# A decoder block's down phases: left factors pinned in VectorE's order, GpSimd taken out of the first down phase, the last product's operands loaded during three products

## The chip, the core and the metric

The kernel runs on one core of a Trainium2 chip: TensorE (PE, matrix products), VectorE (DVE) and ScalarE (ACT) and GpSimd (POOL) for element work, and SyncE (SP), whose queue issues nearly all DMA transfers. The metric is the device time of one execution in microseconds (us), the median of several runs.

## The reference

One layer of a decoder: `x` is 2048 tokens by 1024 features in float32. A mixer sub-layer (attention and a gated convolution) comes first and is not touched here. The part that matters is the gated MLP and the closing norm:

```python
h = rms_norm(x, norm2_g[l]) * (1.0 + sc2) + sh2
u = h @ w_up[l]                       # 1024 -> 2 * 2816
gate, val = u[..., :D_FF], u[..., D_FF:]
f = jax.nn.silu(causal_dwconv3(gate, ffn_conv_w[l], ffn_conv_b[l])) * val
x = x + g2 * (f @ w_down[l])          # 2816 -> 1024
...
return rms_norm(x, final_norm_g)
```

## The kernel before

After the mixer the 2048 tokens are treated in two halves (`hf` 0 and 1), each with an up phase (`h @ w_up`) and a down phase (`f @ w_down`): up 0, down 0, up 1, down 1. Every matrix product is done with seven block products instead of eight, and every float32 operand is split into a rounded high part (written by ScalarE, line 337) and the rest (a subtraction on VectorE or GpSimd, line 338), so that one logical matmul is three of TensorE's.

**Left factors.** An up phase needs 28 tiles `S`, its left factors: for each of four values of `kp`, seven sums and differences of normed activations, each split in two. `left_steps` makes them. For the second half they are made during down 0: it loads four tiles of `x1d` (the residual in DRAM) into `u`, `ta`, `ta` and `tb`, scales them with the norm (line 772), forms sums and differences (777, 782, 785, and 788 on GpSimd), and splits them (758, 759; for two of the seven the split's second part is on GpSimd). `beside`, called once in each step of down 0, advances this generator.

**Down phase.** It has seven products (`i` 0 to 6) of 11 steps (`k`). A step takes a pair of tiles `op` (high and low parts, each with a left block and a right block) made by `down_step`: two loads of 256 KB into a tile `wr` (lines 1095, 1096), the high part on ScalarE, the low part on VectorE or, for each fourth step, on GpSimd. There are 3 tiles `wr` and 8 tiles `op` (four pairs). The pair of a step is asked for three steps ahead (`AHEAD`). A step is 12 matmuls into four PSUM banks. The last product of down 1 differs: its eleven pairs go into tiles of the tag `S` (28 of them, no longer needed by then), all are kept, and TensorE goes through them bank by bank. They are asked for after the last step's pair of product 5, since `todo` is one list in order of `i` and `k`.

**Closing norm.** `final` squares and sums the finished columns, `rstd_cols` makes 1/rms, `spread2` spreads it over the partitions with a matmul into the one PSUM bank `aux`, copies it by ScalarE (739) into a tile, and line 1118 multiplies eight tiles with it and sends them out.

**Order.** TensorE's instructions stay in the order of the program (`keep_in_program_order`). Those of the other engines are put in an order at build time by a scheduler that weighs them against its own estimates; at run time each engine and the SP queue go strictly through their lists.

Of the kernel before, what the change touches and what calls it, by code (L numbers as in the profile page):

```python
# [8 lines left out]
F32 = mybir.dt.float32  # L9
# [3 lines left out]
ALU = mybir.AluOpType  # L13
# [7 lines left out]
T = 512  # L21
# [36 lines left out]
def build(nc, tc, cst, pp, dr, xT, pos, pk_d, c_d, ada_d, w_in, w_o, w_up, w_dn, outT):  # L58
# [7 lines left out]
    def mm(*a, **k):  # L66
        i = nc.tensor.matmul(*a, **k)  # L67
        if static[0]:
            tc.keep_in_program_order(i)
# [662 lines left out]
    def spread2(r4, tag, gtag='nq'):  # L732
        g = t(gtag)
        vec.tensor_tensor(out=g.rearrange("p (m t) -> p m t", m=4), in0=ident.unsqueeze(1).to_broadcast([128, 4, 128]),
                          in1=r4.unsqueeze(2).to_broadcast([128, 4, 128]), op=ALU.mult)
        p = aux_tile()
        mm(p, ones, g, start=True, stop=True)
        r = t(tag)
        act(r, p, AF.Copy)
        return r  # L740
# [8 lines left out]
    def left_steps(hf, SL, rb=None):  # L749
        for n in ('11', 's1', '12', 's2', 's4', 's3', '22'):  # L750
            SL[n] = []

        def put(n, src, bias=None):
            o = t('S', dt=F32R)
            if bias is None or rb is None:
                split(o[:, W], o[:, L], src, pool if n in ('s4', 's3') and rb is not None else vec)
            else:
                act(o[:, W], src, AF.Identity, bias=bias)
                vec.scalar_tensor_tensor(out=o[:, L], in0=src, scalar=bias, in1=o[:, W].bitcast(F32),  # L759
                                         op0=ALU.add, op1=ALU.subtract)  # L760
            SL[n].append(o)

        for kp in range(4):
            A = {}
            b0, b1, b01 = sh2[:, kp:kp + 1], sh2[:, kp + 4:kp + 5], sh12[:, kp:kp + 1]
            for n, b, hk, tag in (('11', 0, 0, 'u'), ('21', 1, 0, 'ta'), ('22', 1, 1, 'ta'), ('12', 0, 1, 'tb')):
                k = kp + 4 * hk
                a = A[n] = t(tag)
                c0 = (2 * hf + b) * T
                dma(a, (h2d if rb is None else x1d)[k][:, c0:c0 + T])  # L770
                if rb is not None:
                    vec.scalar_tensor_tensor(out=a, in0=a, scalar=s2[:, k:k + 1], in1=rb[b], op0=ALU.mult, op1=ALU.mult)
                if n == '11':
                    put('11', a, b0)
                yield
            z = t('tb')
            vec.tensor_tensor(out=z, in0=A['21'], in1=A['22'], op=ALU.add)
            put('s1', z, b01)
            yield
            put('12', A['12'], b1)  # L780
            yield
            vec.tensor_tensor(out=z, in0=z, in1=A['11'], op=ALU.subtract)
            put('s2', z, b1)
            yield
            vec.tensor_tensor(out=A['12'], in0=A['12'], in1=z, op=ALU.subtract)
            put('s4', A['12'])
            yield
            (vec if rb is None else pool).tensor_tensor(out=A['21'], in0=A['11'], in1=A['21'], op=ALU.subtract)
            put('s3', A['21'])
            yield  # L790
            put('22', A['22'], b1)
            yield
# [15 lines left out]
    for q in range(NQ):  # L808
# [81 lines left out]
        for dp in range(4):  # L890
            if dp == 3:
                ps += [ps_tile(tg) for tg in ('pv', 'ps')]
                out_half(q, ps, 0, 3, ya8)
            out_half(q, ps, 1, dp, yc8)
            for d in (2 * dp, 2 * dp + 1):
                out_res(q, ps[d], d, ss2)
                if q == NQ - 1:
                    for _ in range(5):
                        next(ls, None)
    out_pool.close()  # L900
    right_pool, _ = open_pool("fb", "left", {'op': (1024, 8), 'x2': (512, 8), 'nq': (512, 2), 'wr': (1024, 3)})
# [196 lines left out]
        split(hi, lo, raw, eng)  # L1098
        return hi, lo

    def final(hf, b, x2, tag, rtag):
        s = t(tag)
        order = [(d + 4 * b) % 8 for d in range(8)]
        for i, d in enumerate(order):
            if i == 0:
                act(s, x2[d], AF.Square)
            else:
                q = t(tag)
                act(q, x2[d], AF.Square)
                vec.scalar_tensor_tensor(out=s, in0=q, scalar=EPS * D / 128 if i == 1 else 0.0, in1=s,  # L1110
                                         op0=ALU.add, op1=ALU.add)
            yield
        r = rstd_cols(s, D)
        yield
        r = spread2(r, rtag, tag)
        yield
        for d in order:
            vec.scalar_tensor_tensor(out=x2[d], in0=x2[d], scalar=col('gf', d), in1=r, op0=ALU.mult, op1=ALU.mult)  # L1118
            c0 = (2 * hf + b) * T
            dma(outT[d][:, c0:c0 + T], x2[d])  # L1120
            yield
# [3 lines left out]

    def down_phase(hf, hook, ops):

        todo = [(i, k) for i in range(7) for k in range(KH)][len(ops):]
        count = itertools.count()

        def nxt():
            if todo:
                ops.append(down_step(hf, *todo.pop(0), pool if next(count) % 4 == 3 else vec))

        for _ in range(AHEAD - len(ops)):
            nxt()
        out = {}, {}
        fin = [final(hf, 0, out[0], 'u', 'u'), final(hf, 1, out[1], *(('nq', 'nq') if hf == 0 else ('ta', 'tb')))]
        sets = [None, None]
        reads = []  # L1140

# [4 lines left out]
        n = 0  # L1146
        for i, (st, _, _, c) in enumerate(DOWN):
# [11 lines left out]
            for k in range(KH):  # L1159
                if at_end:  # L1160
                    break
                hi, lo = ops.pop(0)
                for p in range(4):
                    wc = slice(T + p * 128, T + (p + 1) * 128)
                    mm(ps[p], hi[:, wc], hi[:, W], start=(fresh and k == 0), stop=False, skip_group_check=True)
                    mm(ps[p], hi[:, wc], lo[:, W], start=False, stop=False, skip_group_check=True)
                    mm(ps[p], lo[:, wc], hi[:, W], start=False, stop=(k == KH - 1 and i in (1, 5, 6)),
                       skip_group_check=True)
                if reads:
                    read(*reads.pop(0))  # L1170
                nxt()
                if hf == 1 and i == 5:
                    nxt()
                if i == 2 and 5 <= k < 9 or i == 6:
                    next(fin[0], None)
                if i == 6 and k >= 6:
                    next(fin[0], None)
                if i == 5 and 5 <= k < 9:
                    next(fin[1], None)
                hook(n)  # L1180
                n += 1
            reads, done = [(ps[p], c, p) for p in range(4)], reads
        if hf == 1:
            while todo:
                nxt()
            for p in range(4):
                wc = slice(T + p * 128, T + (p + 1) * 128)
                for k, (hi, lo) in enumerate(ops):
                    mm(ps[p], hi[:, wc], hi[:, W], start=False, stop=False, skip_group_check=True)
                    mm(ps[p], hi[:, wc], lo[:, W], start=False, stop=False, skip_group_check=True)  # L1190
                    mm(ps[p], lo[:, wc], hi[:, W], start=False, stop=(k == KH - 1), skip_group_check=True)
# [30 lines left out]
    SL, R = {}, {}  # L1222
    rs = right_steps(0, R)
    ls = []
    NLEFT = 44

    def beside(n):
        if n == 2:
# [81 lines left out]
```

## Time and profile before

| what | us |
|---|---|
| median of 3 runs (2240.96 to 2241.58) | 2240.99 |
| the profiled execution's own time | 2238.82 |
| its span, first to last instruction | 2237.0 |
| TensorE busy in the span | 2058.7 |
| VectorE busy | 1592.7 |
| GpSimd busy | 532.9 |

The profile is of one execution, 2.17 us below the median; its time is 1.8 us more than its span. TensorE is busy for 92% of the span, so what can be won is mostly in the places where it waits, and in the stretches after such waits in which its clock is low.

### The profile page before, as it was taken

The numbers are of one execution on the slowest core, as the hardware profiler recorded it, in microseconds if no ns is written. First come the engines' busy times: TensorE is split into PE (matmuls) and PEld (weight loads), VectorE is DVE, ScalarE is ACT, GpSimd is POOL, SyncE is SP. The second block draws the span as 40 slices with busy tenths as digits, with TensorE's granted clock in tenths as the row PEclk, the third lists the DMA queues.
The fourth block names the chain that finished last, engine by engine and source line by source line (L and its number), as shares of the span: only waits on it lengthen the run. The fifth ranks groups of instructions, "written<-read, shape, count | busy, mean of one in ns | idle before, by whom it ended". The sixth has DMA issues, their size and how long they took to land.

```text
span 2237.0 us, 26087 instructions
## 1 busy us (share of the span) xinstructions
PE 2058.7 (92%) x8914; PEld 1646.0 (74%) x8914; DVE 1592.7 (71%) x2589; ACT 985.9 (44%) x1719; POOL 532.9 (24%) x306
## 2 busy tenths in 40 slices
PE   4877968988998997999999998999999999999996
PEld 3765757766777775877887877787788888878874
DVE  8897548747854759888888868758877777654454
ACT  3564435435533534544444434544544444434341
POOL 5264410000000001323323323423232323212220
PEclk7998989999999998999999999999999999999997
DMA  7674776677667556545345566665433232256662
GB/s 284 208 257 144 268 252 244 231 255 249 213 215 241 171 177 228 181 149 178 138 172 171 188 202 191 195 198 178 156 104 109 90 112 100 99 175 201 190 203 97
DMA packets 164918, 414.80 MB, mean 185 GB/s; under 512 B 19248, under 2 KB 23344, under 8 KB 152240
## 3 DMA queue, kind: packets, MB, share of 16 engines
q1 hardware_dynamic: 164640, 413.02, 54.5%
q8 instruction: 70, 1.15, 0.2%
q14 instruction: 64, 0.52, 0.1%
q10 hardware_dynamic: 144, 0.11, 0.0%
HBM read 304.52 MB, written 100.93 MB: 181 GB/s over the span
## 4 chain that ended last, share of the span: by engine, by line
PE 44%; DVE 4%; DMA 3%; issue 1%; ACT 1%; SPq 0%; POOL 0%; DVEq 0%; ACTq 0%; POOLq 0%
PE ps L67 21%; PE sc L67 12%; PE tr L67 7%; PE aux L67 2%; PE pv L67 1%; DVE op L338 1%; DMA wr<-tt 1%; DVE S L759 1%; DMA u<-x1d 0%; DMA wr<-w_dn 0%; ACT op L337 0%; DMA tb<-x1d 0%; DMA y<-x1d 0%; DVE x L1118 0%; DMA f<-u 0%
## 5 line engine op out<-in xcount | busy, mean ns | idle before, releaser
L338 POOL TENSOR_TENSOR op<-wr,op 128x512 fp32r<-128x512 f32 (+1 forms) x123 | 240.3, 1954 | 1221.6 <-DVE o L338 585.9
L67 PE MATMUL ps<-h,w 128*128 128x512 f32 x1632 | 425.6, 411 | 37.1 <-ACT rq L496 15.1
L67 PE MATMUL ps<-S,op 128*128 128x512 f32 x1584 | 389.9, 399 | 21.8 <-ACT op L337 11.5
L67 PEld LDWEIGHTS ps<-h,w 128*128 128x128 f32 x1632 | 311.3, 195 | 115.6 <-ACT rq L496 17.7
L67 PEld LDWEIGHTS ps<-S,op 128*128 128x128 f32 x1584 | 299.1, 189 | 98.8 <-ACT op L337 14.7
L337 ACT ACTIVATE op<-wr 128x1024 fp32r<-128x1024 f32 (+1 forms) x229 | 205.1, 896 | 254.6 <-PE sc L67 85.2
L338 DVE TENSOR_TENSOR op<-wr,op 128x1024 fp32r<-128x1024 f32 x106 | 140.4, 1327 | 135.8 <-ACT op L337 135.8
L1007 DVE SCALAR_TENSOR_TENSOR u<-G,pk,u 128x512 f32<-128x512 f32 x176 | 156.5, 891 | 34.2 <-ACT u L1004 32.6
L67 PE MATMUL sc<-S,op 128*128 128x512 f32 x528 | 131.0, 397 | 0.0
L67 PE MATMUL ps<-S,o 128*128 128x512 f32 x528 | 130.4, 395 | 0.0
L67 PE MATMUL tr<-S,op 128*128 128x512 f32 x528 | 130.3, 395 | 0.0
L67 PE MATMUL sc<-S,o 128*128 128x512 f32 x528 | 130.3, 395 | 0.0
L67 PE MATMUL ps<-op 128*128 128x512 f32 x462 | 120.0, 394 | 9.1 <-DVE op L338 4.8
L67 PE MATMUL sc<-op 128*128 128x512 f32 x462 | 118.4, 392 | 0.0
L67 PEld LDWEIGHTS sc<-S,op 128*128 128x128 f32 x528 | 99.8, 189 | 24.3
L67 PEld LDWEIGHTS sc<-S,o 128*128 128x128 f32 x528 | 99.1, 188 | 24.1
L67 PEld LDWEIGHTS tr<-S,op 128*128 128x128 f32 x528 | 99.1, 188 | 24.1
L67 PEld LDWEIGHTS ps<-S,o 128*128 128x128 f32 x528 | 99.0, 188 | 24.0
L67 PEld LDWEIGHTS ps<-op 128*128 128x128 f32 x462 | 86.6, 188 | 29.5 <-DVE op L338 5.6
L1004 ACT ACTIVATE u<-G,pk 128x512 f32<-128x512 f32 x88 | 71.4, 812 | 82.4 <-DVE G L988 80.7
L338 POOL TENSOR_TENSOR w<-wr,w 128x1024 fp32r<-128x1024 f32 x28 | 74.3, 2662 | 137.3 <-ACT w L337 116.3
L337 ACT ACTIVATE op<-ta 128x512 fp32r<-128x512 f32 x132 | 81.0, 624 | 57.6 <-PE ps L67 51.8
(315 smaller groups left out, 3533.6 us busy)
## 6 DMA issues: line engine op xcount, KB each, us to landing
w<-wd SPq DMA_DIRECT2D x72, 1024.0 KB, 5.9
wr<-w_up SPq DMA_DIRECT2D x86, 512.0 KB, 3.3
wd<-w SPq DMA_DIRECT2D x26, 1024.0 KB, 5.4
fs<-u SPq DMA_DIRECT2D x88, 256.0 KB, 2.1
wr<-fs SPq DMA_DIRECT2D x88, 256.0 KB, 2.9
wr<-tt SPq DMA_DIRECT2D x88, 256.0 KB, 3.3
f<-u SPq DMA_DIRECT2D x66, 256.0 KB, 2.0
wr<-f SPq DMA_DIRECT2D x66, 256.0 KB, 2.9
```

Of the source, the lines that this page charges most:

```text
L67: i = nc.tensor.matmul(*a, **k)
L337: act(hi, src, AF.Copy)
L338: return lo_eng.tensor_tensor(out=lo, in0=src, in1=hi.bitcast(F32), op=ALU.subtract)
L759: vec.scalar_tensor_tensor(out=o[:, L], in0=src, scalar=bias, in1=o[:, W].bitcast(F32), op0=ALU.add, op1=ALU.subtract)
L1004: act(u, G[:, 2:], AF.Identity, scale=fwh[:, 2 * NFF + j:2 * NFF + j + 1], bias=fwh[:, 3 * NFF + j:3 * NFF + j + 1])
L1007: vec.scalar_tensor_tensor(out=u, in0=G[:, i:i + T], scalar=fwh[:, i * NFF + j:i * NFF + j + 1], in1=u, op0=ALU.mult, op1=ALU.add)
```

## The change

Three things. The second half's left factors: every VectorE instruction of them is pinned in program order, nothing of them is on GpSimd any more, and the four loads of a `kp` are issued one `kp` ahead; the number of `yield`s falls (so `NLEFT` is 41 instead of 44). Down 0: all low parts on VectorE. Down 1: the eleven pairs of the last product have a list of their own and are asked for in every third step of products 3, 4 and 5. Besides, `spread2` returns the PSUM bank when it is given no tag, and `final` multiplies straight from it.

```diff
@@ spread2 @@
         mm(p, ones, g, start=True, stop=True)
+        if tag is None:
+            return p
         r = t(tag)
@@ left_steps @@
             if bias is None or rb is None:
-                split(o[:, W], o[:, L], src, pool if n in ('s4', 's3') and rb is not None else vec)
+                keep(split(o[:, W], o[:, L], src, vec))
             else:
                 act(o[:, W], src, AF.Identity, bias=bias)
-                vec.scalar_tensor_tensor(out=o[:, L], in0=src, scalar=bias, in1=o[:, W].bitcast(F32),
-                                         op0=ALU.add, op1=ALU.subtract)
+                keep(vec.scalar_tensor_tensor(out=o[:, L], in0=src, scalar=bias, in1=o[:, W].bitcast(F32),
+                                              op0=ALU.add, op1=ALU.subtract))
             SL[n].append(o)
+        def keep(x):
+            return x if rb is None else tc.keep_in_program_order(x)
+
+        def load(kp):
+            A = {}
+            for n, b, hk, tag in (('11', 0, 0, 'u'), ('21', 1, 0, 'ta'), ('22', 1, 1, 'ta'), ('12', 0, 1, 'tb')):
+                A[n] = t(tag)
+                c0 = (2 * hf + b) * T
+                dma(A[n], (h2d if rb is None else x1d)[kp + 4 * hk][:, c0:c0 + T])
+            return A
+
+        nxt = load(0)
+        yield
         for kp in range(4):
-            A = {}
+            A = nxt
...
-            vec.tensor_tensor(out=A['12'], in0=A['12'], in1=z, op=ALU.subtract)
+            if kp < 3:
+                nxt = load(kp + 1)
+            keep(vec.tensor_tensor(out=A['12'], in0=A['12'], in1=z, op=ALU.subtract))
             put('s4', A['12'])
             yield
-            (vec if rb is None else pool).tensor_tensor(out=A['21'], in0=A['11'], in1=A['21'], op=ALU.subtract)
+            keep(vec.tensor_tensor(out=A['21'], in0=A['11'], in1=A['21'], op=ALU.subtract))
             put('s3', A['21'])
@@ final @@
-        r = spread2(r, rtag, tag)
+        r = spread2(r, None, tag)
@@ down_phase @@
-        todo = [(i, k) for i in range(7) for k in range(KH)][len(ops):]
+        todo = [(i, k) for i in range(7 - hf) for k in range(KH)][len(ops):]
+        last = [(6, k) for k in range(KH)] if hf == 1 else []
+        lops = []
...
-                ops.append(down_step(hf, *todo.pop(0), pool if next(count) % 4 == 3 else vec))
+                ops.append(down_step(hf, *todo.pop(0), pool if hf == 1 and next(count) % 4 == 3 else vec))
...
                 nxt()
-                if hf == 1 and i == 5:
-                    nxt()
+                if last and i >= 3 and k % 3 == 0:
+                    lops.append(down_step(hf, *last.pop(0), pool if len(lops) % 4 == 2 else vec))
...
-            while todo:
-                nxt()
+            assert not last
...
-                for k, (hi, lo) in enumerate(ops):
+                for k, (hi, lo) in enumerate(lops):
```

Up to the first steps of down 0 all engines' lists are the same as before, and TensorE's list is the same from end to end. The lists differ at three places. The first is VectorE at the start of down 0 (`op<-wr` is a step's low part, lines 772, 777 and 759 the left factors). Before:

```order
L338 TENSOR_TENSOR op<-wr,op 128x1024 x2
L772 SCALAR_TENSOR_TENSOR tb<-tb,s_105,u 128x512
L772 SCALAR_TENSOR_TENSOR ta<-ta,s_105,u 128x512 x4
L772 SCALAR_TENSOR_TENSOR u<-u,s_105 128x512
L777 TENSOR_TENSOR tb<-ta 128x512
L772 SCALAR_TENSOR_TENSOR u<-u,s_105 128x512
L777 TENSOR_TENSOR tb<-ta 128x512
L338 TENSOR_TENSOR op<-wr,op 128x1024
L772 SCALAR_TENSOR_TENSOR tb<-tb,s_105,u 128x512
L759 SCALAR_TENSOR_TENSOR S<-u,sh_106,S 128x512
```

The same place in the changed kernel (lines 785 and 761 are the former 772 and 759, 1162 is the former 1144, which reads a finished PSUM bank):

```order
L338 TENSOR_TENSOR op<-wr,op 128x1024 x6
L785 SCALAR_TENSOR_TENSOR u<-u,s_105 128x512
L338 TENSOR_TENSOR op<-wr,op 128x1024
L785 SCALAR_TENSOR_TENSOR ta<-ta,s_105,u 128x512
L761 SCALAR_TENSOR_TENSOR S<-u,sh_106,S 128x512
L338 TENSOR_TENSOR op<-wr,op 128x1024 x2
L785 SCALAR_TENSOR_TENSOR ta<-ta,s_105,u 128x512
L1162 SCALAR_TENSOR_TENSOR y_10668<-ps,g_107,y_10668 128x512
L338 TENSOR_TENSOR op<-wr,op 128x1024
L785 SCALAR_TENSOR_TENSOR tb<-tb,s_105,u 128x512
```

Before, nine instructions of the left factors, of two values of `kp` at once, stand between two low parts; now they come one to five at a time, over the whole phase.

The second place is SP's queue in down 0, where `ta<-x1d` are left factors' loads and `wr<-` those of the steps. In the changed kernel the loads of the third `kp` stand behind the fourth step of product 2:

```order
L1111 DMA wr<-fs_115 128x512
L1112 DMA wr<-tt_126 128x512
L773 DMA ta<-x1d 128x512 x2
L1111 DMA wr<-fs_115 128x512
L1112 DMA wr<-tt_126 128x512
```

Before, the same pair of loads stood in the middle of product 1:

```order
L770 DMA ta<-x1d 128x512
L1095 DMA wr<-f_112 128x512
L1096 DMA wr<-w_dn 128x512
L770 DMA ta<-x1d 128x512
```

They moved back by about a product, while VectorE's use of them moved back by more: in the changed list it stands behind the low part of step 40 of 77, and the loads behind that of step 25.

The third place is VectorE in products 3 to 6 of down 1 (`S<-wr` is a low part of the last product). Before, all of them stand behind the last low part of product 5:

```order
L1110 SCALAR_TENSOR_TENSOR ta<-ta 128x512 x3
L338 TENSOR_TENSOR op<-wr,op 128x1024 x6
L338 TENSOR_TENSOR S<-wr,S 128x1024 x3
L1144 SCALAR_TENSOR_TENSOR y_16284<-tr,g_107,y_16284 128x512
```

In the changed kernel they stand among those of products 3, 4 and 5 (those missing between the rows are GpSimd's):

```order
L338 TENSOR_TENSOR op<-wr,op 128x1024
L338 TENSOR_TENSOR S<-wr,S 128x1024
L338 TENSOR_TENSOR op<-wr,op 128x1024 x2
L338 TENSOR_TENSOR S<-wr,S 128x1024
L338 TENSOR_TENSOR op<-wr,op 128x1024 x5
L338 TENSOR_TENSOR S<-wr,S 128x1024
L1162 SCALAR_TENSOR_TENSOR x_16516<-tr,g_107,x_16516 128x512
```

The loads and ScalarE's high parts moved with them: 40 pairs pass the three `wr` tiles in 29 steps.

## Rows read from the trace of the kernel before

**Rows 1.** The page's busy times over the span: us, share, instructions.

```profile
PE 2058.7 (92%) x8914; PEld 1646.0 (74%) x8914; DVE 1592.7 (71%) x2589; ACT 985.9 (44%) x1719; POOL 532.9 (24%) x306
```

**Rows 2.** Busy time by stretch: down 0, down 1's products 0-5, product 6, the tail.

```profile
core 0: us, PE busy (x) PEld busy (x) DVE busy (x) ACT busy (x) POOL busy (x), PEclk, DMA share, GB/s
1318.49:1551.05 232.56, 218.79 (x939) 177.41 (x937) 166.74 (x162) 107.83 (x126) 74.35 (x34) 0.98 0.64 204
...
1993.50:2171.51 178.01, 178.01 (x787) 147.41 (x786) 82.28 (x77) 73.27 (x73) 38.77 (x16) 1.00 0.65 207
2171.51:2198.68 27.17, 21.50 (x67) 14.14 (x66) 14.43 (x17) 12.49 (x14) 4.72 (x2) 0.81 0.40 127
2198.68:2237.00 38.32, 21.94 (x87) 16.06 (x85) 17.63 (x32) 3.32 (x7) 0.00 (x0) 0.77 0.31 110
```

**Rows 3.** TensorE's timeline in down 0: start, us, operation, idle time before and its releaser.

```profile
1349.51 1.43 PE L67 MATMUL ps<-op 128*128 128x512 f32 x5 [1.86 <-DVE op L338]
...
1365.23 2.50 PE L67 MATMUL tr<-op 128*128 128x512 f32 x5 [4.53 <-DVE op L338]
...
1369.84 1.56 PE L67 MATMUL tr<-op 128*128 128x512 f32 x6
...
1422.14 1.43 PE L67 MATMUL ps<-op 128*128 128x512 f32 x5 [2.92 <-DVE op L338]
```

**Rows 4.** VectorE's timeline at the first two of these waits.

```profile
1346.06 4.53 DVE L338 TENSOR_TENSOR op<-wr,op 128x1024 fp32r<-128x1024 f32 x2
...
1361.97 3.21 DVE L338 TENSOR_TENSOR op<-wr,op 128x1024 fp32r<-128x1024 f32 x1
```

**Rows 5.** GpSimd's timeline at the same two waits.

```profile
1345.94 2.43 POOL L338 TENSOR_TENSOR op<-wr,op 128x1024 fp32r<-128x1024 f32 x1 [1.69 <-ACT op L337]
...
1361.76 2.34 POOL L338 TENSOR_TENSOR op<-wr,op 128x1024 fp32r<-128x1024 f32 x1 [6.54 <-ACT op L337]
```

**Rows 6.** VectorE's groups by shape in 1995 to 2165 (down 1): busy us, mean ns, idle before.

```profile
L338 DVE TENSOR_TENSOR op<-wr,op 128x1024 fp32r<-128x1024 f32 x47 | 58.9, 1254 | 83.8 <-ACT op L337 83.8
...
L1144 DVE SCALAR_TENSOR_TENSOR y<-tr,g,y 128x512 f32<-128x512 f32 x2 | 1.5, 746 | 1.1 <-PE tr L67 1.1
```

**Rows 7.** VectorE's groups by shape in 1322 to 1425 (first part of down 0).

```profile
L338 DVE TENSOR_TENSOR op<-wr,op 128x1024 fp32r<-128x1024 f32 x22 | 34.5, 1574 | 10.8 <-ACT op L337 10.8
...
L777 DVE TENSOR_TENSOR tb<-ta 128x512 f32<-128x512 f32 x4 | 2.7, 681 | 0.0
```

**Rows 8.** GpSimd's groups by shape in 1318 to 1553 (down 0).

```profile
L338 POOL TENSOR_TENSOR op<-wr,op 128x1024 fp32r<-128x1024 f32 x18 | 45.0, 2499 | 141.1 <-ACT op L337 141.1
L788 POOL TENSOR_TENSOR ta<-u,ta 128x512 f32<-128x512 f32 x4 | 9.1, 2280 | 6.5 <-DVE tb L777 4.5 <-DVE u L772 1.9
L338 POOL TENSOR_TENSOR S<-tb,S 128x512 fp32r<-128x512 f32 x4 | 7.1, 1776 | 16.8 <-ACT S L337 16.8
L338 POOL TENSOR_TENSOR S<-ta,S 128x512 fp32r<-128x512 f32 x4 | 6.5, 1633 | 0.0
```

**Rows 9.** The chain that ended last: a load of a left factor's tile.

```profile
1352.76 5.80 DMA tb<-x1d
```

**Rows 10.** TensorE's timeline around down 1's last product.

```profile
2168.79 1.52 PE L67 MATMUL tr<-op 128*128 128x512 f32 x6
...
2171.51 2.48 PE L67 MATMUL ps<-S 128*128 128x512 f32 x10
...
2176.68 0.96 PE L67 MATMUL ps<-S 128*128 128x512 f32 x3 [1.55 <-POOL S L338]
...
2198.68 0.95 PE L67 MATMUL aux<-ones,u 128*128 128x2 f32 x8
```

**Rows 11.** ScalarE's timeline: a high part of a step in down 1.

```profile
2155.39 1.06 ACT L337 ACTIVATE op<-wr 128x1024 fp32r<-128x1024 f32 x1 [1.61 <-PE aux L67]
```

**Rows 12.** SP's queue: first loads of four of the last pairs.

```profile
2166.33 0.32 SPq L1095 DMA_DIRECT2D wr<-f  x1
...
2168.18 0.37 SPq L1095 DMA_DIRECT2D wr<-f  x1
...
2178.51 0.32 SPq L1095 DMA_DIRECT2D wr<-f  x1
...
2182.33 0.32 SPq L1095 DMA_DIRECT2D wr<-f  x1
```

**Rows 13.** Groups by shape in the tail, 2200 to 2237.

```profile
L1118 DVE SCALAR_TENSOR_TENSOR x<-x,pk,tb 128x512 f32<-128x512 f32 x8 | 5.4, 747 | 2.9 <-ACT tb L739 2.9
...
L739 ACT ACTIVATE tb<-aux 128x512 f32<-128x512 f32 x1 | 0.6, 597 | 3.8 <-PE aux L67 3.8
```

More of the change, by code (lines that the diff above doesn't have):

```diff
@@ L755, in put @@
             if bias is None or rb is None:
-                split(o[:, W], o[:, L], src, pool if n in ('s4', 's3') and rb is not None else vec)
+                keep(split(o[:, W], o[:, L], src, vec))
             else:
                 act(o[:, W], src, AF.Identity, bias=bias)
-                vec.scalar_tensor_tensor(out=o[:, L], in0=src, scalar=bias, in1=o[:, W].bitcast(F32),
-                                         op0=ALU.add, op1=ALU.subtract)
+                keep(vec.scalar_tensor_tensor(out=o[:, L], in0=src, scalar=bias, in1=o[:, W].bitcast(F32),
+                                              op0=ALU.add, op1=ALU.subtract))
             SL[n].append(o)
+        def keep(x):
[9 more added lines that the diff above has]
+        yield
         for kp in range(4):
-            A = {}
+            A = nxt
             b0, b1, b01 = sh2[:, kp:kp + 1], sh2[:, kp + 4:kp + 5], sh12[:, kp:kp + 1]
-            for n, b, hk, tag in (('11', 0, 0, 'u'), ('21', 1, 0, 'ta'), ('22', 1, 1, 'ta'), ('12', 0, 1, 'tb')):
+            for n, b, hk in (('11', 0, 0), ('21', 1, 0), ('22', 1, 1), ('12', 0, 1)):
                 k = kp + 4 * hk
-                a = A[n] = t(tag)
-                c0 = (2 * hf + b) * T
-                dma(a, (h2d if rb is None else x1d)[k][:, c0:c0 + T])
+                a = A[n]
                 if rb is not None:
-                    vec.scalar_tensor_tensor(out=a, in0=a, scalar=s2[:, k:k + 1], in1=rb[b], op0=ALU.mult, op1=ALU.mult)
+                    keep(vec.scalar_tensor_tensor(out=a, in0=a, scalar=s2[:, k:k + 1], in1=rb[b], op0=ALU.mult, op1=ALU.mult))
                 if n == '11':
                     put('11', a, b0)
-                yield
+                if rb is not None or n == '11':
+                    yield
             z = t('tb')
-            vec.tensor_tensor(out=z, in0=A['21'], in1=A['22'], op=ALU.add)
+            keep(vec.tensor_tensor(out=z, in0=A['21'], in1=A['22'], op=ALU.add))
             put('s1', z, b01)
@@ L781, in left_steps @@
             yield
-            vec.tensor_tensor(out=z, in0=z, in1=A['11'], op=ALU.subtract)
+            keep(vec.tensor_tensor(out=z, in0=z, in1=A['11'], op=ALU.subtract))
             put('s2', z, b1)
             yield
-            vec.tensor_tensor(out=A['12'], in0=A['12'], in1=z, op=ALU.subtract)
+            if kp < 3:
+                nxt = load(kp + 1)
+            keep(vec.tensor_tensor(out=A['12'], in0=A['12'], in1=z, op=ALU.subtract))
             put('s4', A['12'])
             yield
-            (vec if rb is None else pool).tensor_tensor(out=A['21'], in0=A['11'], in1=A['21'], op=ALU.subtract)
+            keep(vec.tensor_tensor(out=A['21'], in0=A['11'], in1=A['21'], op=ALU.subtract))
             put('s3', A['21'])
@@ L897, in build @@
                 if q == NQ - 1:
-                    for _ in range(5):
+                    for _ in range(3):
                         next(ls, None)
@@ L1099, in down_step, with final @@
         return hi, lo
-    def final(hf, b, x2, tag, rtag):
+    def final(hf, b, x2, tag):
         s = t(tag)
@@ L1137, in down_phase @@
         out = {}, {}
-        fin = [final(hf, 0, out[0], 'u', 'u'), final(hf, 1, out[1], *(('nq', 'nq') if hf == 0 else ('ta', 'tb')))]
+        fin = [final(hf, 0, out[0], 'u'), final(hf, 1, out[1], 'nq' if hf == 0 else 'ta')]
         sets = [None, None]
@@ L1224, in build @@
     ls = []
-    NLEFT = 44
+    NLEFT = 41
     def beside(n):
```

## The prediction

> **What bounds the kernel.** First the page's busy times: TensorE is busy for 92% of the span, every other engine far less [rows 1]. So the span is TensorE's work plus its waits plus what a low clock costs behind a wait. The table by stretch says where those are: down 0 takes 232.56 us of which TensorE is idle for 13.8; products 0 to 5 of down 1 hold no idle time at all (178.01 of 178.01); product 6 takes 27.17 us at a mean granted clock of 0.81; the tail is 38.32 us [rows 2]. The change leaves TensorE's list as it is, so only waits and clock can move.
>
> A step of a down phase is 12 matmuls and takes 2.72 us at full clock: the last step of product 5 starts at 2168.79 and product 6 at 2171.51 [rows 10]. That is 0.227 us a matmul.
>
> In TensorE's timeline of down 0 three waits name a low part on VectorE (line 338): 1.86, 4.53 and 2.92 us, 9.31 together [rows 3]. Behind the longest, the eleven matmuls from 1365.23 to 1369.84 took 4.61 us instead of 2.49, so the low clock cost 2.1 more. What made the low parts late is seen by laying VectorE beside GpSimd: at 1361.97 a low part took 3.21 us, and two from 1346.06 on took 4.53 [rows 4], while a GpSimd low part ran from 1361.76 for 2.34 and from 1345.94 for 2.43 [rows 5]. Undisturbed the same instruction takes 1.25 us (47 of them, down 1), in the first part of down 0 it took 1.57 [rows 6, 7]. And it stood behind nine instructions of the left factors, as the lists show.
>
> **Part 1, down 0.** GpSimd loses 18 low parts, 4 subtractions and 8 second parts of left factors, 67.7 us of its time [rows 8]. VectorE gets them: 18 x 1.25 + 12 x 0.68 = 30.7 us [rows 6, 7]. It was busy for 166.7 us of the 232.6 [rows 2], some of that stretched by GpSimd (22 low parts x 0.32 = 7 us alone), so it comes to at most 197 us, against 77 steps x 2.72 = 209 us of TensorE. It does not become the bound on the mean. What counts is lateness: a low part may begin three steps ahead of its use, 8.16 us, of which the high part takes 1.06 [rows 11] and the low part 1.25; 5.8 us are free. In the new list never more than five short instructions (3.8 us at 0.75) stand between two low parts (before, up to nine), except at the very end, where the eight multiplications of the norm stood before too. So I expect all three waits gone: 9.3 + 2.1 = **-11.4**. The bounds: 0 if VectorE stays late, -11.4 if not; I take the far end, since the largest block between low parts falls below what is free.
>
> [...]
>
> The left factors' loads: pinned instructions wait in order, and with them all low parts behind. A load of a tile took 5.80 us [rows 9]. In SP's new list the third `kp`'s loads stand behind step 25's, their use behind step 40's low part: 15 steps of 2.72, 41 us. No price.
>
> **Part 2, the norm.** ScalarE's copy of 0.60 us [rows 13] leaves the path in front of the last eight multiplications: 0.60 and its hand-over, **-0.65**. They now read PSUM. The nearest row is line 1144, the same operation with one PSUM operand: 746 ns against 747 from SBUF alone [rows 6, 13], so nothing is paid back. The first `final` of down 0 gains the same ahead of up 1, where VectorE then has other work in its list: between 0 and -0.6, I take **-0.3**.
>
> [...]
>
> **Part 3, product 6 of down 1.** It waits since its pairs are asked for last: a step's high part waits for TensorE to free its `op` pair [rows 11], and the last product's loads stand behind. 66 matmuls x 0.227 = 14.96 us would do, it takes 27.17 (one of its waits in [rows 10]): **-12.2** when all eleven pairs are ready.
>
> The price is in products 3 to 5, where TensorE never waited. 40 pairs in 29 steps: one per 29 x 2.72 / 40 = 1.97 us, through three `wr` tiles. How fast can these turn? After 2166, where no pair waits for TensorE any more, SP's loads show it: a tile is loaded again when its split is done, so 2166.33 to 2178.51 are two turns, 6.09 us each, and 2168.18 to 2182.33 two turns with one GpSimd split among them, 7.08 each [rows 12]. Three tiles: 2.03 and 2.36 us a pair. Bounds of what falls behind in 40 pairs: 40 x 0.06 = 2.4, which the free 5.8 us swallow, so 0; and 40 x 0.39 = 15.6, less 5.8, so 9.8 of waiting. A quarter of the pairs (7 + 3) stay on GpSimd. Taking a turn with it as 2 x 7.08 - 6.09 = 8.07, the mean is 0.75 x 6.09 + 0.25 x 8.07 = 6.59, 2.20 a pair: 40 x 0.23 = 9.2 behind, less 5.8, less the lead of the ring when it starts (3 x (2.72 - 2.20) = 1.6): I take **+2**, nearer to the low end, since the lag is largest only at the end of the stretch.
>
> **Sum.** 11.4 + 0.3 + 0.65 + 12.2 - 2 = 22.5 us. The profiled execution took 2238.82, so 2216.3; the median shown is 2.17 above it: **2218.5**. The first half's left factors and both up phases: same lists or same places, 0.
>
> **Rivals.** (a) The three tiles cannot carry 40 pairs in 29 steps; TensorE now waits in products 4 and 5 for an `op` pair: the 9.8 instead of 2, 2226. For it: 1.97 is below even the best turn measured, 2.03. Against: the lag must first use up 5.8 us, and the extra pairs stop with step 6 of product 5. (b) VectorE stays late in down 0, as its list is now in order and has 30.7 us more: the 11.4 stay, 2230. For it: its load rises to some 0.85 of the phase. Against: the spacing in the list, and that each instruction gets shorter without GpSimd. (c) Both, with a low clock behind each new wait (2.1 us was the cost once): 22.5 - 7.8 - 11.4 - 2.1 leaves 1.2, 2240: nothing measurable has come of it. (d) Slower: a pinned instruction of the left factors waits for its load, in each of the four `kp`, and all low parts queue behind it. Each wait costs TensorE what exceeds 5.8 us; it decides from (22.5 + 4.5) / 4 = 6.8 us per `kp` on, so a load that is 12.6 us late; at 15 us late four times 9.2 = 37, 2255. For it: VectorE did wait for such a load, and one took 5.80 [rows 9]. Against: 41 us of lead in the list.
>
> **Numbers.** About 0.2% (4.5 us) is what can be told from no change. Forecast 0.64 (2214 to 2223), (a) 0.15, (b) 0.09, (c) 0.06, (d) 0.06. The first three make it faster: 0.88; same 0.06, slower 0.06. The forecast's own low end is all waits gone and nothing paid, 2216.5, less 2 for the low clock elsewhere; the range goes up over (a) and (b) to 2230: 2214 to 2230.
>
> **What would show it.** In TensorE's timeline of the changed down 0: no wait for line 338 over 1 us, and the stretch at about 221 us (232.6 - 11.4). VectorE's low parts there at 1.2 to 1.3 us, GpSimd empty until up 1's first weights. Product 6 in 15 us with no wait, clock 1.0. In products 4 and 5 waits for an `op` pair of 0 to 4 us in all. The last multiplications directly behind TensorE's spread, 0.75 us each. I am wrong if VectorE waits for `x1d` loads in down 0, if ScalarE's high parts in products 4 and 5 wait for `wr` loads by more than 6 us, or if up 1 starts later behind the last low part of down 0.

## The result: 2220.6 us, 0.9% faster

The changed kernel takes 2220.6 us (median of four runs, 2219.0 to 2221.4); the kernel before took 2241.3 beside it. The ratio is 0.990 with a 95% interval of 0.9883 to 0.9917. The profiled execution has a span of 2217.3 us against 2237.0, so 19.7 us less. The predicted time was 2218.5, in a range from 2214 to 2230.

The page of the changed kernel: TensorE does the same 8914 matmuls, and GpSimd has 276 instructions in place of the 306 of [rows 1].

```profile
PE 2052.7 (93%) x8914; PEld 1646.0 (74%) x8914; DVE 1588.5 (72%) x2619; ACT 985.0 (44%) x1715; POOL 470.6 (21%) x276
```

The same stretches as in [rows 2], in the changed kernel: down 0, products 0 to 5 of down 1, product 6, the tail (the last line ends 0.1 us before the span does).

```profile
core 0: us, PE busy (x) PEld busy (x) DVE busy (x) ACT busy (x) POOL busy (x), PEclk, DMA share, GB/s
1319.75:1538.90 219.15, 215.43 (x939) 176.28 (x937) 164.84 (x194) 108.76 (x127) 7.19 (x3) 0.99 0.67 216
1978.58:2165.98 187.40, 182.12 (x787) 147.90 (x786) 90.53 (x86) 82.62 (x83) 43.49 (x18) 0.99 0.67 214
2165.98:2180.99 15.01, 15.01 (x67) 12.38 (x66) 4.96 (x8) 3.44 (x5) 0.00 (x0) 1.00 0.00 0
2180.99:2217.20 36.21, 20.32 (x87) 15.19 (x85) 17.57 (x32) 2.12 (x5) 0.00 (x0) 0.81 0.33 117
```

Laid beside [rows 2] line by line, and with what lies between the lines, this is where the 19.7 us came from:

| stretch | before | after | difference | predicted |
|---|---|---|---|---|
| ahead of down 0 | 1318.49 | 1319.75 | +1.3 | 0 |
| down 0 | 232.56 | 219.15 | -13.4 | -11.4 |
| up 1, its start included | 442.45 | 439.68 | -2.8 | -0.3 |
| products 0 to 5 of down 1 | 178.01 | 187.40 | +9.4 | +2 |
| product 6 | 27.17 | 15.01 | -12.2 | -12.2 |
| tail | 38.32 | 36.31 | -2.0 | -0.65 |

The gains came out 5.9 us larger than forecast and the losses 8.7 us larger, 7.4 of them in products 0 to 5 of down 1; the two nearly cancel.

**Down 0.** VectorE's groups there: busy us, mean ns, idle before.

```profile
L338 DVE TENSOR_TENSOR op<-wr,op 128x1024 fp32r<-128x1024 f32 x74 | 90.4, 1223 | 48.6 <-ACT op L337 48.5
L761 DVE SCALAR_TENSOR_TENSOR S<-tb,sh,S 128x512 fp32r<-128x512 f32 x12 | 8.7, 747 | 0.0
L1134 DVE SCALAR_TENSOR_TENSOR y<-y,pk,aux 128x512 f32<-128x512 f32 x8 | 5.3, 740 | 0.0
```

All 74 low parts take 1.22 us in the mean, where the first 22 took 1.57 [rows 7]. VectorE is idle for 48.5 us only because it waits for ScalarE's high parts; so it is early, not late. GpSimd does nothing here until 1531.7; its 7.19 us are up 1's first weights. TensorE's timeline of this stretch holds no wait for line 338 at all, where [rows 3] has three of them. The multiplications of the norm, which now read PSUM, take 0.740 us.

**Down 1.** TensorE's timeline, products 3 to 6: start, us, operation, idle time before and its releaser.

```profile
2110.95 1.40 PE L67 MATMUL ps<-op 128*128 128x512 f32 x5 [0.76 <-DVE op L338]
...
2129.37 1.45 PE L67 MATMUL ps<-op 128*128 128x512 f32 x5 [1.21 <-POOL op L338]
...
2138.63 1.45 PE L67 MATMUL tr<-op 128*128 128x512 f32 x5 [0.77 <-DVE op L338]
...
2145.56 1.42 PE L67 MATMUL tr<-op 128*128 128x512 f32 x5 [1.12 <-DVE op L338]
...
2155.16 1.42 PE L67 MATMUL tr<-op 128*128 128x512 f32 x5 [1.14 <-POOL op L338]
...
2165.98 15.17 PE L67 MATMUL ps<-S 128*128 128x512 f32 x66
```

Product 6 runs through: 66 matmuls in one row, where [rows 10] has waits. In front of it, all in products 4 and 5, stand five waits of 5.0 us together, with shorter ones beside them. Before the change there was none. What is behind them is in the engines' own waits over 2060 to 2156 (engine, line, waited for: us in total, times, longest); first ScalarE's high parts, then SP's loads:

```profile
ACT op L337 <- DMA wr<-tt: 16.9, 15, 2.3
ACT op L337 <- DMA wr<-w_dn: 10.7, 8, 2.6
ACT S L337 <- DMA wr<-tt: 9.2, 10, 1.5
```

```profile
SPq L1111 <- DVE op L338: 31.7, 23, 2.6
SPq L1111 <- POOL op L338: 17.4, 8, 3.1
SPq L1111 <- DVE S L338: 8.0, 8, 1.7
SPq L1111 <- POOL S L338: 1.7, 1, 1.7
SPq L1111 <- DMA wr<-tt: 1.2, 1, 1.2
```

It is a closed circle: the high part waits for the load into a `wr` tile, and the load waits until the split of that tile's last pair is done. Before, the high part waited for TensorE to free an `op` pair [rows 11]. So the ring of three tiles had become the bound of this stretch. Of its 9.4 us some 1.5 are not the ring's: behind a wait of 2.1 us the first six matmuls of down 1 took 2.76 us in place of 1.52, at a granted clock of 0.50 (1978.56 to 1981.12). One and the same kernel shows this start in one run and not in another: in the kernel with two edits in down 1, which was run twice (below), these six took 1.55 us in one profile and 2.73 in the other. That leaves 7.9.

**Tail.** TensorE's spread and the last eight multiplications behind it:

```profile
2205.94 2.05 PE L67 MATMUL aux<-ta,ones 128*128 128x512 f32 x2 [1.96 <-DVE ta L734]
```

```profile
2208.03 5.36 DVE L1134 SCALAR_TENSOR_TENSOR x<-x,pk,aux 128x512 f32<-128x512 f32 x8 [2.23 <-PE aux L67]
```

VectorE starts 0.04 us after TensorE ends, and needs 5.36 us for eight, as in [rows 13].

### The profile page after: what moved, and what is told of

Read it like the earlier page. It is cut to its first block, busy times and chain, and to the rows that moved or that the text cites. A ratio compares the mean times of both kernels' runs of the same rounds, so it can differ in the third digit from the quotient of the medians.

```text
span 2217.3 us, 26062 instructions
## 1 busy us (share of the span) xinstructions
PE 2052.7 (93%) x8914; PEld 1646.0 (74%) x8914; DVE 1588.5 (72%) x2619; ACT 985.0 (44%) x1715; POOL 470.6 (21%) x276
## 4 chain that ended last, share of the span: by engine, by line
PE 46%; DMA 2%; DVE 2%; ACT 1%; issue 1%; POOL 0%; SPq 0%; DVEq 0%; ACTq 0%; POOLq 0%
PE ps L67 22%; PE sc L67 13%; PE tr L67 7%; PE aux L67 2%; PE pv L67 1%; DMA wr<-tt 1%; DMA wr<-w_dn 1%; ACT op L337 1%; DVE op L338 1%; POOL op L338 0%; DVE S L338 0%; DVE x L1134 0%; ACT S L337 0%; SPq L1111 0%; DVE u L1023 0%
## 5 line engine op out<-in xcount | busy, mean ns | idle before, releaser
L338 POOL TENSOR_TENSOR op<-wr,op 128x512 fp32r<-128x512 f32 (+1 forms) x105 | 196.9, 1875 | 1295.9 <-ACT op L337 1261.9
L338 DVE TENSOR_TENSOR op<-wr,op 128x1024 fp32r<-128x1024 f32 x124 | 152.1, 1227 | 129.9 <-ACT op L337 128.0
L67 PE MATMUL tr<-op 128*128 128x512 f32 x396 | 101.4, 390 | 3.0 <-DVE op L338 1.9
```

The lines of the kernel that those rows point to most:

```text
L338: return lo_eng.tensor_tensor(out=lo, in0=src, in1=hi.bitcast(F32), op=ALU.subtract)
```

## The experiments

Ten edits of the changed kernel were run, and two kernels once more. The time ahead of down 0 differs by more than 8 us between runs with the same lists up to there (down 0 began at 1317.4 in one and 1326.0 in another), so the kernels are compared by stretches; the medians are given beside them. Four marks are used, all on TensorE's timeline: the first matmuls of down 0, of up 1 and of down 1 (its `sc` rows), and product 6. By them, down 0 with up 1's start took 234.9 us before (1318.49 to 1553.41) and 219.4 in the changed kernel; down 1's products 0 to 5 took 178.2 and 187.4.

### What bounds products 3 to 5

**No GpSimd split in down 1.**

```
-                ops.append(down_step(hf, *todo.pop(0), pool if hf == 1 and next(count) % 4 == 3 else vec))
+                ops.append(down_step(hf, *todo.pop(0), vec))
...
-                    lops.append(down_step(hf, *last.pop(0), pool if len(lops) % 4 == 2 else vec))
+                    lops.append(down_step(hf, *last.pop(0), vec))
```

Expected: 

> The changed kernel with all low parts of down 1 on VectorE (GpSimd has none, neither of the steps nor of the last product). In the changed kernel products 0 to 5 took 187.40 us against 178.01 before; of the 9.4 some 1.5 lie at their start, 7.9 are waits in products 3 to 5. Theory (the ring of three wr tiles is the bound, and a GpSimd split makes a turn of 8.07 us out of one of 6.09): a pair costs 2.03 us against 1.97 demanded, 40 x 0.06 = 2.4 behind, less than the 5.8 that are free; products 0 to 5 fall to about 180 us and the time to about 2213. Rival 1 (the transfers or SP's issue bound the ring, whoever splits): 187 and 2220. Rival 2 (VectorE becomes late, 10 more low parts x 1.25 us in the 87 us of products 3 to 5): over 187, waits that name line 338 on VectorE, 2222 or more.

Measured: 2219.8 us (ratio 0.9896, 0.9883 to 0.9909). Products 0 to 5 took 183.7 us. TensorE's waits there:

```profile
2130.26 1.42 PE L67 MATMUL tr<-op 128*128 128x512 f32 x5 [0.16 <-DVE op L338]
2136.84 1.45 PE L67 MATMUL tr<-op 128*128 128x512 f32 x5 [0.46 <-DVE op L338]
2146.08 1.43 PE L67 MATMUL tr<-op 128*128 128x512 f32 x5 [0.73 <-DVE op L338]
2155.44 1.43 PE L67 MATMUL tr<-op 128*128 128x512 f32 x5 [0.75 <-DVE op L338]
```

Halfway: counted from the start of down 1 the first comes 23 us later than in the changed kernel, the stretch is 3.7 us shorter, but the waits are not gone. Counted by SP's loads, the ring turned over a pair in 2.23 us (40 pairs, 39 distances, from 2061.54 to 2148.65), against 2.30 in the changed kernel (from 2066.78 to 2156.32). So a quarter of the splits on GpSimd costs the ring 0.07 us a pair in the mean, and without them the ring is still far from the 2.03 that was expected.

**The last pairs asked for in products 0 to 5.**

```
-                if last and i >= 3 and k % 3 == 0:
+                if last and k % 5 == 2:
```

Expected: 

> The changed kernel with the eleven pairs of the last product asked for in products 0 to 5 (two to a product) in place of 3 to 5; GpSimd keeps its quarter. Theory (the ring's rate is the bound): 68 pairs in 57 steps are one per 57 x 2.72 / 68 = 2.28 us against a mean of 2.20 that the prediction took for the ring (2.31 as it came out: (29 x 2.72 + 7.9 + 5.8) / 40), so little or nothing falls behind: products 0 to 5 at 180 us, time 2213 to 2215. Rival (each extra pair has a fixed price of 7.9 / 11 = 0.7 us wherever it stands, by its transfers or by its splits on ScalarE and VectorE): 187 us, 2220.

Measured: 2220.8 us (0.9906, 0.989 to 0.9921); products 0 to 5 took 185.3, of which 1.6 is a slow start. Five waits are listed, 3.6 us, three of them for GpSimd. By the mean this should not be. What happens is seen at one of them, in SP's queue and then in ScalarE's timeline:

```profile
2104.23 0.32 SPq L1111 DMA_DIRECT2D wr<-fs  x1
...
2105.32 0.32 SPq L1111 DMA_DIRECT2D wr<-f  x1
...
2106.45 0.32 SPq L1111 DMA_DIRECT2D wr<-fs  x1
...
2112.31 0.32 SPq L1111 DMA_DIRECT2D wr<-fs  x1
```

```profile
2109.97 1.06 ACT L337 ACTIVATE S<-wr 128x1024 fp32r<-128x1024 f32 x1 [5.35 <-DMA wr<-tt]
```

GpSimd held one tile until 2104.2, the two tiles after it were free by then or soon after, and the loads of three pairs went out within 2.6 us. They were then under way together, ScalarE waited 5.35 us for one of them, and the next pair's loads came only 5.9 us after the third's. Here the tiles move in a bunch, so the mean distance of the pairs is not what decides. The expectation for this kernel was wrong on that point.

**Both together.** The two edits above in one kernel.

Expected: 

> Both at once: the last product's pairs asked for in products 0 to 5, and no GpSimd split in down 1. Ring theory: 2.28 us demanded, 2.03 to be had: no wait at all, products 0 to 5 at 178 to 180 us, time 2211 to 2213, at or just under the better of the two alone. Rival (the price is fixed per extra pair, or lies in VectorE's time): 187 us or more, 2220 or more.

Measured: 2218.3 us (0.9886, 0.9871 to 0.9902). Products 0 to 5 took 178.9 us, with a single listed wait of 0.19 us:

```profile
2129.75 1.45 PE L67 MATMUL ps<-op 128*128 128x512 f32 x5 [0.19 <-DVE op L338]
...
2162.34 15.17 PE L67 MATMUL ps<-S 128*128 128x512 f32 x66
```

So the price has two factors, the distance of the pairs and GpSimd's hold on a tile: 7.9 with both, 3.9 without GpSimd and 5.5 with the pairs spread (slow starts taken off), under 1 with none. A fixed price per extra pair is out, and so is VectorE's time, since VectorE has most to do here.

**Tiles of their own for the last product's operands.** The same eleven pairs, loaded into `tb` tiles, which are free by then:

```
+        if hf == 1 and i == 6:
+            ra, rb = t('tb'), t('tb')
+            dma(ra, fd[hf][l][k])
+            dma(rb, td[r][k])
+            hi, lo = t(tag, dt=F32R), t(tag, dt=F32R)
+            split(hi[:, W], lo[:, W], ra, eng)
+            split(hi[:, L], lo[:, L], rb, eng)
+            return hi, lo
```

Expected: 

> The changed kernel with the last product's operands loaded into tiles of their own (128x512, two for a pair) in place of the ring of three wr tiles; the scheduler then puts their 22 loads at the start of down 1, between those of its first pairs. The ring carries the regular pairs alone, GpSimd keeps its quarter. Theory (the three tiles are what limits): one pair in 2.72 us is easy for a ring that turns a pair in 2.3, no wait in products 1 to 5, these 178 to 180 us, the time 2213. Rival 1 (ScalarE's and VectorE's time for the splits, or the transfers themselves, are the limit): the waits stay in some place, 187. Rival 2 (22 loads ahead of the second and third pair make the first steps of down 1 late, by up to 22 x 1 us of their queue): more lost at the start of down 1 than the ring gives back, 2222 or more.

Measured: 2220.7 us (0.9908, 0.9885 to 0.9931). Products 0 to 5 took 179.0 us without one wait, GpSimd's quarter included. But all 22 loads now go out from 1963.21 to 2005.12, and the splits of these pairs with them, so products 3 to 5 were rid of the eleven pairs' transfers and splits, and not only of their place in the ring: this run does not tell the three apart. For the tiles speak the waits of the two queues above, where in 2060 to 2156 SP waits 58.8 us for splits and 1.2 for anything else. Rival 2 holds too. Before down 1's first steps TensorE now waits 6.5 us instead of 2.1; by their place in the lists the 22 loads and their splits are the likely cause, which was not tried further:

```profile
1980.69 1.65 PE L67 MATMUL ps<-op 128*128 128x512 f32 x3 [6.51 <-DVE u L1034]
```

**Part 3 undone.**

```
-        todo = [(i, k) for i in range(7 - hf) for k in range(KH)][len(ops):]
-        last = [(6, k) for k in range(KH)] if hf == 1 else []
-        lops = []
+        todo = [(i, k) for i in range(7) for k in range(KH)][len(ops):]
...
-                if last and i >= 3 and k % 3 == 0:
-                    lops.append(down_step(hf, *last.pop(0), pool if len(lops) % 4 == 2 else vec))
+                if hf == 1 and i == 5:
+                    nxt()
...
```

Expected: 

> Part 3 of the change undone alone: the last product's pairs are asked for last again, two per step from product 5 on, as before the change; parts 1 and 2 stay. Theory: product 6 back to 27.2 us (+12.2), products 3 to 5 without their waits (-7.9): 2220.6 + 4.3 = 2224.9. Rival (the waits in products 3 to 5 come from parts 1 and 2, or from a later start, and not from the extra pairs): they stay, and the time is 2220.6 + 12.2 = 2232.8.

Measured: 2227.6 us (0.9934, 0.9921 to 0.9947). Products 0 to 5 took 179.8 (1.6 of it a slow start) with no wait, product 6 took 28.0. Part 3 is worth 13.0 in product 6 and costs 7.6 in front of it. Its net is 5.3 by the stretches, and the waits in products 3 to 5 belong to the extra pairs alone.

### What emptied down 0

Part 1 does three things there: it takes 30 instructions from GpSimd, it keeps VectorE's left factors in program order, and it loads their tiles one `kp` earlier. Four kernels take the first two apart; all four keep the third.

**GpSimd's low parts back, order kept**: `pool if next(count) % 4 == 3 else vec` in the step's line.

Expected: 

> The changed kernel with every fourth low part of down 0 on GpSimd again; the left factors stay on VectorE and in program order. It parts the two halves of part 1. The changed kernel's down 0 takes 219.15 us, before it took 232.56. Theory (lateness comes from instructions of VectorE and GpSimd that stretch one another, and from the block of nine between low parts, about alike): VectorE's low parts longer again (1.25 to 1.6 us in the mean, some over 3), some waits for line 338 come back, 2 to 8 us: down 0 at 221 to 227. Rival 1 (it was the order alone): 219, all waits stay gone. Rival 2 (it was GpSimd alone): near 232. Where up 1 starts, GpSimd's last low parts of down 0 would stand in its way again only if they are near the end: up 1's start (439.68 us in the changed kernel, 442.45 before) within 0.5 of the changed kernel.

Measured: 2222.2 us (0.990, 0.9885 to 0.9916); down 0 with up 1's start 220.6, no wait for line 338. What is left are 1.32 us ahead of the norm's spread, in place of 0.67, and 0.60 at up 1's start.

**Order not kept, GpSimd still out**: `keep` gives `x` back as it is.

Expected: 

> The changed kernel with the left factors free to move in VectorE's list, as before the change; they stay on VectorE, and GpSimd stays out of down 0. The other half of part 1. Theory (both halves count): the low parts keep their 1.25 us, but a block of left factors (now twelve more instructions) between two low parts makes some late: 2 to 8 us of waits, down 0 at 221 to 227. Rival 1 (it was GpSimd alone): 219, no wait. Rival 2 (the order alone, and the list is now worse than before since VectorE has 30 us more): 232 or more.

Measured: 2228.1 us (0.993, 0.9914 to 0.9947); 222.3 us, three waits for low parts, though these take 1.22 us each:

```profile
1348.92 1.45 PE L67 MATMUL ps<-op 128*128 128x512 f32 x5 [0.58 <-DVE op L338]
...
1362.41 1.43 PE L67 MATMUL tr<-op 128*128 128x512 f32 x5 [2.28 <-DVE op L338]
...
1374.20 1.45 PE L67 MATMUL tr<-op 128*128 128x512 f32 x5 [0.24 <-DVE op L338]
```

In front of the longest, VectorE has ten short instructions of 0.7 us between two low parts, none of them stretched:

```profile
1353.50 1.23 DVE L338 TENSOR_TENSOR op<-wr,op 128x1024 fp32r<-128x1024 f32 x1 [0.51 <-ACT op L337]
...
1361.14 1.22 DVE L338 TENSOR_TENSOR op<-wr,op 128x1024 fp32r<-128x1024 f32 x1
```

**GpSimd's left factors back** (4 subtractions, 8 second parts), order kept, low parts on VectorE:

```
-                keep(split(o[:, W], o[:, L], src, vec))
+                if n in ('s4', 's3') and rb is not None:
+                    split(o[:, W], o[:, L], src, pool)
+                else:
+                    keep(split(o[:, W], o[:, L], src, vec))
...
-            keep(vec.tensor_tensor(out=A['21'], in0=A['11'], in1=A['21'], op=ALU.subtract))
+            (keep(vec.tensor_tensor(out=A['21'], in0=A['11'], in1=A['21'], op=ALU.subtract)) if rb is None else
+             pool.tensor_tensor(out=A['21'], in0=A['11'], in1=A['21'], op=ALU.subtract))
```

Expected: 

> The changed kernel with GpSimd's share of the left factors back (4 subtractions and 8 second parts, as before the change); the low parts stay on VectorE, VectorE's share of the left factors stays in program order. Down 0 from its first matmuls to up 1's first: 234.92 us before, 219.44 in the changed kernel, 220.62 with GpSimd's low parts back, 222.30 without the pinned order. Theory (the pinned order makes what GpSimd takes from VectorE harmless, since no more than five instructions stand between two low parts): 219.5 to 221.5, waits for line 338 under 1 us in all. Rival (the 15.5 us came from these twelve instructions, the longest dependent chain between the two engines): 225 or more.

Measured: 2219.4 us, one run; 217.9 us, no wait for line 338.

**All of it back on GpSimd, order kept**: this edit and the first one together, so against the kernel before the order is new, with the earlier loads.

Expected: 

> All that part 1 took from GpSimd in down 0 is back on GpSimd (18 low parts, 4 subtractions, 8 second parts); what is left of the left factors on VectorE is still in program order. So the order alone is changed against the kernel before. Theory (the order does the most, the work taken from GpSimd little): the stretch at 220 to 224 us. Rival (the two only do it together; with GpSimd as busy as before the instructions stretch one another as before): 228 to 235, waits of 2 us and more for line 338.

Measured: 2225.7 us, one run; 220.7 us, no wait for line 338. VectorE's groups in this down 0:

```profile
L338 DVE TENSOR_TENSOR op<-wr,op 128x1024 fp32r<-128x1024 f32 x56 | 74.2, 1326 | 50.4 <-ACT op L337 50.4
L764 DVE SCALAR_TENSOR_TENSOR S<-tb,sh,S 128x512 fp32r<-128x512 f32 x12 | 14.2, 1203 | 2.2 <-ACT S L763 2.2
L764 DVE SCALAR_TENSOR_TENSOR S<-u,sh,S 128x512 fp32r<-128x512 f32 x4 | 8.4, 2101 | 2.7 <-ACT S L763 2.7
```

VectorE's instructions are again longer with GpSimd at work beside them (a second part takes 1.2 to 2.1 us in place of 0.75), but the longer ones are now above all those of the left factors, for which TensorE does not wait there.

| down 0 with up 1's start, us | left factors in the scheduler's order | in program order |
|---|---|---|
| GpSimd has its share | 234.9 (before) | 220.7 |
| GpSimd has none | 222.3 | 219.4 (the change) |

Either half alone gives 12.6 or 14.2 of the 15.5 us. The cells scatter by the start of down 0: behind its first wait the first six `sc` matmuls took 2.58 us in the kernel before, 2.46 in the change and 2.76 in the 220.7 cell, but 1.53 in the 222.3 cell; the granted clock was 0.54 in the first two (1321.59 to 1325.34 and 1322.84 to 1326.58). That is worth 1.6 us (kernels with the changed kernel's own down 0 took 217.9 twice and 219.2 to 219.5 six times, the change among them), so counted alike the half without GpSimd gives 11.0, and the 217.9 of the kernel above is no gain over 219.4. A long block of short instructions alone still makes a low part late (2.28 us); with a low part stretched to 3.21 us behind seven of them the wait was 4.53 [rows 3, 4].

One thing is common to all the cells but the first: the left factors' tiles are loaded one `kp` earlier. That alone was not tried. Against it: in the 222.3 cell VectorE still waits for such a load (2.3 us for `u`), and before, only one such wait stands directly ahead of a late low part, of 1.03 us:

```profile
1358.65 0.75 DVE L772 SCALAR_TENSOR_TENSOR tb<-tb,s,u 128x512 f32<-128x512 f32 x1 [1.03 <-DMA tb<-x1d]
```

### The norm's copy

```
-        r = spread2(r, None, tag)
+        r = spread2(r, 'u' if b == 0 else ('nq' if hf == 0 else 'tb'), tag)
```

Expected: 

> The changed kernel with ScalarE's copy after the norm's spread back in both down phases (part 2 undone alone). Theory: 0.63 us more between TensorE's spread and the last eight multiplications, which then read SBUF and take as long as from PSUM (0.74 to 0.75 us); tail 36.3 + 0.6, and of the 2.8 us that up 1's start gained nothing or at most 0.6 lost: time 2220.6 + 0.6 to 1.2, not to be told from the changed kernel by the time alone. [...] Rival 2 (the gain at up 1's start comes from part 2: without the copy VectorE's multiplications there are over earlier): 439.68 goes back to about 442.4.

Measured: 2227.3 us (0.9928, 0.9909 to 0.9947). In the tail the multiplications start 0.67 us after the spread (2214.24 to 2214.91) in place of 0.04, and take the same:

```profile
2214.91 5.39 DVE L1134 SCALAR_TENSOR_TENSOR x<-x,pk,tb 128x512 f32<-128x512 f32 x8 [2.86 <-ACT tb L741]
```

That is 0.63, as forecast, with nothing paid back from PSUM (5.39 us for eight from SBUF, 5.36 from PSUM). Up 1's first matmuls waited 0.32 us in place of none, not 2.36. Up 1 took 2.7 us longer; its timeline has one new wait that accounts for it, 2.54 us at 1588.24 for line 1011, far behind the copy. Another kernel without the copy had 0.93 at this place, so whether the copy brings it is open. The median is 6.7 us above that of the changed kernel and 3.2 above its second measurement (below); the 0.63 and the 2.7 are what its stretches show, the rest lies where the edit touches nothing.

### The two once more, side by side

The changed kernel as it is: 

> The changed kernel as it is, once more, to have its time and its stretches beside the next kernel on one chip. Down 0 219 to 220 us, products 0 to 5 of down 1 187 us, time 2219 to 2222.

The kernel with the two edits in down 1: 

> The kernel with the last product's pairs in products 0 to 5 and no GpSimd split in down 1, once more, beside the changed kernel. Products 0 to 5 took 178.85 us in it against 187.42. Theory (the 8.6 us show in the time): 5 to 9 us below the changed kernel's median. Rival (what the waits gave back is lost elsewhere, in the tail, where its clock was low: from product 6 to the end it took 54.2 us against 51.3): 2 to 3 us below it or none.

Measured on one chip: 2224.1 us (0.9891, 0.9871 to 0.9911) and 2215.7 (0.9866, 0.9839 to 0.9894). Products 0 to 5 took 187.9 and 179.4. The difference in the stretch shows in both pairs of profiles (8.6 and 8.5 us); in the medians of the two pairs of measurements the second kernel is 2.3 and 8.4 us below the changed one, and its intervals overlap those of the changed kernel. Part of it goes back in the tail, which took 39.1 us in both profiles of this kernel, at a granted clock of 0.75, against 36.3 at 0.81 in both of the changed kernel. This kernel has the lowest median of all that were run; that its whole time is below the change's is likely, but not shown beyond the intervals.

## Why the prediction was right, and which terms were off

**Part 1** was right in its cause, as far as it was parted, and slightly short in size: -13.4 in the stretch against -11.4, all three waits gone, low parts at 1.22 us, GpSimd empty. Rival (b), VectorE late with its 30.7 us more, fell: VectorE's busy time in the stretch even went down, from 166.7 to 164.8 us, since its instructions got shorter (a low part 1.22 us in the mean, where the first 22 had taken 1.57 [rows 7]). Rival (d) did not come: no pinned instruction of this stretch waits for a load. What the prediction did not see is that either half would have been nearly enough. It named the lateness, "behind nine instructions", and the stretching by GpSimd as one story; the table above shows that taking away either one leaves 3.1 us of waits or none of the 9.3. The nine stand ahead of the low part at 1340.19, behind which TensorE did not wait; ahead of the one at 1361.97, which made the longest wait, stand seven short instructions and the 1.03 us for a load, which the prediction left out. That VectorE's instructions get longer with GpSimd at work beside them is seen once more in the 1.2 to 2.1 us of the kernel with all of GpSimd's work back; why they do was not shown. In that kernel TensorE waits for no low part: the time is set by which instruction is hit.

**Up 1's start** was mis-sized, -2.8 against -0.3. Before, its first row waited 2.36 us and then took 4.59 for twelve matmuls; now it waits for nothing and they take 3.04. The prediction counted only the norm's copy there. The runs give 0.32 us of waiting with the copy back, 0.61 with GpSimd's work back and order kept, and none with the order not kept and GpSimd out: here too either half removes most of the 2.36.

**Part 2** was right in the tail: 0.63 measured, 0.65 forecast, nothing paid back from PSUM (a multiplication took 0.740 us from PSUM in down 0, 0.747 from SBUF in [rows 13]). The other 1.4 of the tail are no part of the change: in the four experiments on down 0, whose down 1 is the changed kernel's own, the tail took 37.6 us three times and 38.8 once.

**Part 3** gave its -12.2 exactly. The step that failed is the price, "I take +2": measured 7.9, near the upper bound of 9.8, and rival (a) in its mechanism. The mechanism had been seen, but the turn of 6.09 us, read from SP's loads beside product 6 [rows 12], does not hold in products 3 to 5. One difference is the loads: beside product 6 they took 2.8 and 3.2 us, with 40 pairs in 29 steps they take 3.2 to 3.9, by the medians from issue to landing; first before (2165 to 2185), then after (2060 to 2156):

```profile
wr<-f SPq DMA_DIRECT2D x9, 256.0 KB, 2.8
wr<-tt SPq DMA_DIRECT2D x9, 256.0 KB, 3.2
```

```profile
wr<-tt SPq DMA_DIRECT2D x31, 256.0 KB, 3.8
wr<-fs SPq DMA_DIRECT2D x30, 256.0 KB, 3.2
wr<-f SPq DMA_DIRECT2D x11, 256.0 KB, 3.5
wr<-w_dn SPq DMA_DIRECT2D x10, 256.0 KB, 3.9
```

The load that a split waits for, `tt` or `w_dn`, takes 0.6 to 0.7 us longer, and a turn without GpSimd is 3 x 2.23 = 6.7 us, not 6.09. Why the loads are longer stays open: it is not the amount moved, for the queue carried 219 GB/s in the first window and 221 in the second. With the measured 2.30 a pair the prediction's sum, without its last term of some 1.6 for the lead of the ring, gives 40 x (2.30 - 1.97) - 5.8 = 7.4, and without GpSimd 40 x (2.23 - 1.97) - 5.8 = 4.6, against 7.9 and 3.9 measured. That the two agree roughly is a check of the sum's form and no more, since 2.30 and 2.23 were counted in the stretches whose waits they are to give; for the pairs spread over six products the form does not hold, as the bunch of loads shows.

That the sum came out within 3 us is luck in part: the gains were 5.9 us larger than forecast (2.0 in down 0, 2.5 at up 1's start, 1.4 in the tail) and the losses 8.7 (7.4 in products 0 to 5, 1.3 ahead of down 0): -22.5 forecast, -19.7 measured between the two profiles. The tail's 1.4, the 1.3 ahead of down 0 and 1.5 of the 7.4 lie within what differs between runs of one program.

## What to carry to other kernels

A ring's turn that was read in one stretch need not hold in another: here it was 6.09 us beside product 6 and 6.7, in the mean and without GpSimd, in products 3 to 5, and with so little room that decided the price. Where instructions of one engine get longer beside another's work (here the low parts, 1.57 us against 1.22), it can be enough to see that the longer ones are work for which nobody waits; moving the work away and fixing the order are two cures for one fault, and their gains don't add. And a stretch that never waited has only so much room: count its free time before work is moved into it.

## What was not expected of the hardware

- A load of 256 KB took 2.8 to 3.2 us in the median beside product 6 before (2165 to 2185, 219 GB/s), and 3.2 to 3.9 in 2060 to 2156 of the changed kernel, at 221 GB/s; the loads of three pairs issued within 2.6 us kept ScalarE waiting 5.35.
- The tail's clock differs between runs with the same instructions in it: 0.81 and 36.3 us in the changed kernel twice, 0.75 and 39.1 in the kernel without waits in products 3 to 5 twice, but also 0.75 and 38.8 in the kernel with GpSimd's work back in down 0, whose down 1 is the changed kernel's own. What sets it was not found.
